# Recurrent branch of a hybrid layer: the product of input gate and convolution output on GpSimd instead of VectorE

## The chip, the cores and the metric

The kernel runs on one core of one Trainium2 chip. The metric is the device time of one execution in microseconds (us). The engines are named as in the profile: PE (TensorE), DVE (VectorE), ACT (ScalarE), POOL (GpSimd), SP (SyncE, which issues the DMAs).

## The reference

One layer on 128 context tokens and 1024 latent tokens, 1152 columns in all: a normalised and modulated input goes through one projection into a pooling branch, a recurrent branch and a gate; the two branches are joined by an output projection; a SwiGLU block follows. The change touches the recurrent branch alone:

```
def rg_lru_bidir(xb, w_a, b_a, w_x, b_x, lam, h0):
    ...
    for d in range(N_DIRS):
        r = jax.nn.sigmoid(... xh, w_a[d] ...)
        i = jax.nn.sigmoid(... xh, w_x[d] ...)
        log_a = LRU_C * r * jax.nn.log_sigmoid(lam[d])
        a = jnp.exp(log_a)
        mult = jnp.sqrt(jnp.maximum(-jnp.expm1(2.0 * log_a), 0.0))
        h = linear_scan(a, mult * (i * xb), h0[:, d], reverse=(d == 1))
        ...
```

The product that is moved is `i * xb`: input gate by convolution output. The width of the branch is 512, in four blocks of 128 partitions, and there are two directions, so there are eight such products of 128x1152 float32.

## The kernel before

Channels lie on the partitions and the 1152 tokens on the free axis. The program is not written in the order in which it runs: each piece of work is put into a list with the engines that may do it and a price in us, and a planner (`Sched.run`, printed in part below) sets the order. At each step it takes, over all engines, the piece that could start first by its prices, and among those that could start at once the one that was listed first; a piece that needs a tile waits until a slot of that tile's tag is free. The result is a fixed order for each engine, which the engine follows instruction by instruction: behind one that waits, everything on that engine waits. The helpers `dve`, `tt`, `act`, `pool` and `pe` put a piece on one engine; `anycopy` and `split` leave the choice between ACT and DVE to the planner. The prices come from formulas (`c_dve`: 1.27 us for a product of 1152 columns) or stand in the call.

The recurrent branch is `lru(j)` for j = 0 to 3 (line 647 on). On DVE and ACT it makes the convolution output `xb` (line 659), splits it into a high and a low part `xh`, `xl` (by `split`, lines 309, 311 and 340), multiplies these with the gate weights on PE (line 527, PSUM tile `pt`), and takes the sigmoids on ACT into four `ri` tiles: `rt[d]`, the recurrence gate, and `it[d]`, the input gate. Then for both directions: `a` and a tanh on ACT, a square `sq` (line 702), a product into `rt[d]` (line 704), and the product `it[d]` by `xb` (a `tt`, shown as line 327). A square root on ACT follows, then `it[d]` by `rt[d]` (line 327), the scans (line 719), and their sum.

Around it PE has other work that the planner puts between: the units of the input projection (`gemm_in`, `full_unit`), the modulation (`mod_group`, line 851), and the pooling units (`pool_unit`, whose products on DVE are tiles `C`, `W`, `mix`, with lines 791, 327, 805 to 818). At about 240 us the output projection begins (`gemm_out_mm`, PSUM tiles `ps` and `pm`, line 527), which needs the split `HT`, `LO` of the finished `mix` tiles.

POOL has little to do: memsets of the edges of the tiles `u`, `X` and `C` (lines 550 to 552, 762 to 764, 790), which wait for a free slot of the tag `u`, and between 59 and 68 us some twenty small operations on 128x8 (lines 628 to 640).

Of the kernel before, what the change touches and what calls it, by code (L numbers as in the profile page):

```python
# [11 lines left out]
OP = mybir.AluOpType  # L12
# [4 lines left out]
T = 1152  # L17
# [239 lines left out]
def c_act(n, ps=False, ptr=0):  # L257
    return (("ACT", cp(n, ps) + 0.093 * ptr),)


def c_dve(n, fast=False, ptr=0):
    return (("DVE", 0.068 + n * (0.52 if fast else 1.042) / 1000 + 0.067 * ptr),)
# [10 lines left out]
def kernel(ctx: ExitStack, tc: tile.TileContext, x, cT, vec, rows, w_modA, w_modB, w_in, w_gate,  # L273
                      w_pool, w_out, w_fi, w_fo, y, st_out):
    nc = tc.nc
# [9 lines left out]
    def sb(name, tag="s", shape=(128, T), dt=F32, n=1):  # L285
        return S.buf(tag, lambda: sp.tile(list(shape), dt, name=name, tag=tag, bufs=counts[tag]), n)
# [13 lines left out]
    def act(dst, src, w, r, func=AF.Copy, n=None, ps=False, tset=None, ptr=0, **kw):  # L300
        def fn(e):
            k = {a: (b() if callable(b) else b) for a, b in kw.items()}
            nc.scalar.activation(dst(), src(), func, **k)  # L303
        return S.op(c_act(n, ps, ptr), fn, r, w, tset)
# [18 lines left out]
    def dve(fn, w, r, n, fast=False, ptr=0):  # L323
        return S.op(c_dve(n, fast, ptr), lambda e: fn(), r, w)

    def tt(dst, a, b, w, r, n, op=OP.mult):
        return dve(lambda: nc.vector.tensor_tensor(dst(), a(), b(), op=op), w, r, n)  # L327
# [7 lines left out]
    def pool(fn, w, r, dur):  # L335
        return S.op((("POOL", dur),), lambda e: fn(), r, w)
# [313 lines left out]
    def lru(j):  # L650
        S.tag = f"lru{j}"
        u = us.pop(j)
        xb = sb("xb")
# [35 lines left out]
        for d in range(2):  # L689
            r, i8 = rt[d], d * 4 + j  # L690
            a = av[d] = sb("a")
            act(lambda a=a, r=r: a.t, lambda r=r: r.t, a.all(), r.all() + [("cl",)], AF.Exp, T, tset=EXP, ptr=1,
                scale=cl[:, i8:i8 + 1])
            act(lambda r=r: r.t, lambda r=r: r.t, r.all(), [("cl",)], AF.Tanh, T, tset=TANH, ptr=1,
                scale=ncl[:, i8:i8 + 1])
            sq = sb("sq")

            def square(e, sq=sq, a=a):
                if e == "ACT":
                    nc.scalar.activation(sq.t, a.t, AF.Square)  # L700
                else:
                    nc.vector.tensor_tensor(sq.t, a.t, a.t, op=OP.mult)
            S.op(c_act(T) + c_dve(T), square, a.all(), sq.all())
            dve(lambda r=r, sq=sq: nc.vector.scalar_tensor_tensor(r.t, sq.t, 1.0, r.t, op0=OP.add, op1=OP.mult),
                r.all(), sq.all(), T)
            ig = it[d]
            tt(lambda ig=ig: ig.t, lambda ig=ig: ig.t, lambda: xb.t, ig.all(), xb.all(), T)
        for d in range(2):
            r = rt[d]
            act(lambda r=r: r.t, lambda r=r: r.t, r.all(), [], AF.Sqrt, T, tset=SQ)  # L710
        for d in range(2):
            r, ig, a, i8 = rt[d], it[d], av[d], d * 4 + j
# [185 lines left out]
    for j in range(4):  # L898
        for m in (j, 4 + j):
            if m not in M0:  # L900
                full_unit(m)
        fin(j, lru(j))
        if j == 0:
            mod_group(1)
# [663 lines left out]
```

## Time and profile before

| what | value |
|---|---|
| median of 3 runs | 1091.04 us (1090.93 to 1091.44) |
| time of the profiled execution | 1091.11 us |
| its span in the trace | 1089.3 us |
| mean granted TensorE clock | 0.996 of full speed |
| PE busy | 1071.3 us, 98% |
| DVE busy | 786.7 us, 72% |
| ACT busy | 463.5 us, 43% |
| POOL busy | 10.4 us, 1% |

The span is the time from the first to the last instruction in the trace; 1.8 us of the profiled execution's time lie around it. The profiled execution is 0.07 us above the median.

The busy time over the span in 40 slices of 27.2 us, in tenths:

```profile
PE   7999999999999999999999999999999999999997
...
DVE  5776888996868986658456575574667977878876
ACT  8576858764754333223233232232323233233341
POOL 0020000000000000000000000000000000000000
```

The branch in question lies in slices 3 to 8 (70 to 226 us). Shares of busy time are averages over stages with different limits; what an engine's time is worth is seen from the chain of waits in a stage.

### The profile page before, as it was taken

The page shows a single profiled execution, that of the slowest core. Times are in us where ns is not written, and L with a number is a line of the kernel's source. Part 1 is how long each engine was busy: PE and PEld are TensorE (multiplying, and loading weights), DVE is VectorE, ACT ScalarE, POOL GpSimd, SP SyncE. Part 2 cuts the span into 40 slices and gives each one's busy share as a digit, 9 for nine tenths or more (in the row PEclk, how much of TensorE's full clock was granted, in tenths as well). Part 3 has the DMA queues.
Part 4 walks back from the last instruction along what each step waited for, and adds up shares of the span by engine and source line. Part 5 has one row for each costly group of instructions (what it writes and reads, how often), then busy time and mean ns, then how long its engine had stood idle before and what let it go on. Part 6 is the DMA issues. An engine that isn't in the chain of part 4 may idle for free.

```text
span 1089.3 us, 14667 instructions
## 1 busy us (share of the span) xinstructions
PE 1071.3 (98%) x5708; PEld 920.0 (84%) x5708; DVE 786.7 (72%) x1363; ACT 463.5 (43%) x814; POOL 10.4 (1%) x54
## 2 busy tenths in 40 slices
PE   7999999999999999999999999999999999999997
PEld 6986899988888998888888888888888888888885
DVE  5776888996868986658456575574667977878876
ACT  8576858764754333223233232232323233233341
POOL 0020000000000000000000000000000000000000
PEclk9999999999999999999999999999999999999999
DMA  9868411224413012214223123141237953353622
GB/s 366 305 211 298 150 46 52 78 87 165 139 75 98 20 73 78 111 39 150 84 67 131 72 98 112 39 150 73 78 131 244 377 180 105 85 178 107 203 68 96
DMA packets 47941, 142.09 MB, mean 130 GB/s; under 512 B 4848, under 2 KB 7808, under 8 KB 47872
## 3 DMA queue, kind: packets, MB, share of 16 engines
q1 hardware_dynamic: 47872, 141.17, 37.5%
q8 instruction: 44, 0.72, 0.3%
q14 instruction: 25, 0.20, 0.1%
HBM read 110.06 MB, written 31.08 MB: 130 GB/s over the span
## 4 chain that ended last, share of the span: by engine, by line
PE 92%; DVE 4%; DMA 2%; issue 1%; ACT 1%; SPq 0%; DVEq 0%
PE ps L527 34%; PE ps L1192 30%; PE pm L527 11%; PE pt L527 8%; PE pt L1192 5%; DMA xt<-in_x 1%; PE pm L851 1%; PE pt L460 1%; DVE W L327 1%; DVE C L791 1%; PE pt L490 1%; DVE ri L719 0%; DMA mraw<-in_w_modB 0%; DVE ri L327 0%; DVE ul L340 0%
## 5 line engine op out<-in xcount | busy, mean ns | idle before, releaser
L527 PE MATMUL ps<-bw,au 128*128 128x512 f32 x627 | 164.1, 390 | 0.0
L527 PEld LDWEIGHTS ps<-bw,au 128*128 128x128 f32 x627 | 117.7, 188 | 25.2
L1192 PE MATMUL ps<-T,wu 128*128 128x512 f32 x480 | 117.2, 393 | 0.0
L1192 PE MATMUL ps<-HT,wu 128*128 128x512 f32 x320 | 106.0, 392 | 0.0
L1192 PEld LDWEIGHTS ps<-T,wu 128*128 128x128 f32 x480 | 88.1, 188 | 18.3
L309 ACT ACTIVATE au<-araw 128x512 fp32r<-128x512 f32 x72 | 45.1, 632 | 131.9 <-PE ps L527 80.5
L527 PE MATMUL ps<-HT,uh 128*128 128x384 f32 x280 | 84.9, 345 | 0.0
L527 PE MATMUL ps<-LO,uh 128*128 128x384 f32 x280 | 82.6, 336 | 0.1
L527 PE MATMUL ps<-HT,ul 128*128 128x384 f32 x280 | 82.6, 336 | 0.0
L1192 PEld LDWEIGHTS ps<-HT,wu 128*128 128x128 f32 x320 | 60.1, 188 | 13.2
L1192 PE MATMUL ps<-LO,wu 128*128 128x512 f32 x160 | 62.4, 390 | 0.0
L303 ACT ACTIVATE g<-g 128x512 f32<-128x512 f32 x40 | 25.3, 632 | 83.4 <-DVE g L327 83.2
L309 ACT ACTIVATE wu<-q 128x512 fp32r<-128x512 f32 x60 | 37.8, 629 | 52.7 <-DVE q L327 49.8
L309 ACT ACTIVATE wh<-rw 128x1024 fp32r<-128x1024 f32 x43 | 45.3, 1056 | 31.7 <-DMA rw<-in_w_fi 19.5
L327 DVE TENSOR_TENSOR wu<-q,wu 128x512 fp32r<-128x512 f32 x80 | 54.9, 686 | 2.7 <-ACT wu L309 1.4
L527 PEld LDWEIGHTS ps<-HT,uh 128*128 128x128 f32 x280 | 51.2, 189 | 5.7 <-issue 5.1
L340 DVE TENSOR_TENSOR wl<-rw,wh 128x1024 fp32r<-128x1024 f32 x44 | 53.6, 1219 | 3.0 <-PE ps L1192 2.6
L527 PE MATMUL pt<-bw,au 128*128 128x512 f32 x198 | 54.8, 389 | 0.0
L340 DVE TENSOR_TENSOR au<-araw,au 128x512 fp32r<-128x512 f32 x77 | 51.8, 685 | 1.7 <-ACT au L309 1.3
L527 PEld LDWEIGHTS ps<-LO,uh 128*128 128x128 f32 x280 | 51.9, 189 | 0.3 <-DVE LO L340 0.3
L527 PEld LDWEIGHTS ps<-HT,ul 128*128 128x128 f32 x280 | 51.8, 189 | 0.0
L1192 PE MATMUL ps<-T,wh 128*128 128x512 f32 x160 | 49.5, 391 | 0.0
(322 smaller groups left out, 2357.5 us busy)
## 6 DMA issues: line engine op xcount, KB each, us to landing
rw<-in_w_fi SPq DMA_DIRECT2D x44, 512.0 KB
mraw<-in_w_modB SPq DMA_DIRECT2D x32, 512.0 KB
gdr<-g SPq DMA_DIRECT2D x20, 576.0 KB
araw<-gdr SPq DMA_DIRECT2D x20, 512.0 KB
xt<-in_x SPq DMA_DIRECT2D x18, 512.0 KB
wm<-in_w_modA SPq DMA_DIRECT2D x16, 512.0 KB
rows<-in_w_fo SPq DMA_DIRECT2D x16, 512.0 KB
araw<-sdr SPq DMA_DIRECT2D x15, 512.0 KB
```

The costliest lines, as they stand in the source:

```text
L303: nc.scalar.activation(dst(), src(), func, **k)
L309: nc.scalar.activation(dst(), src(), AF.Copy)
L327: return dve(lambda: nc.vector.tensor_tensor(dst(), a(), b(), op=op), w, r, n)
L340: dve(lambda: nc.vector.tensor_tensor(l(), src(), h().bitcast(F32), op=OP.subtract), w_l, list(r) + list(w_h), n)
L460: nc.tensor.transpose(pt.t[:, i * 128:(i + 1) * 128], xn.t[:, k * 128:(k + 1) * 128], ident)
L490: nc.tensor.matmul(pm.t[32 * j:32 * j + 32, 0:128], sT[:, kt].rearrange("p a b -> p (a b)"), ws[kt // 2].t[:, kt % 2, kind, kk * 128:(kk + ...
L527: nc.tensor.matmul(out, lhsT, rhs, start=first, stop=last)
L791: dve(lambda: nc.vector.tensor_tensor_scan(C.t[:, 1:], ones.to_broadcast([128, PADW - 1]), X.t[:, :PADW - 1], 0.0, op0=OP.mult, op1=OP.add ...
L851: nc.tensor.matmul(pm.t[32 * j:32 * j + 32, 0:256], sT[:, kt].rearrange("p a b -> p (a b)"), raw.t[:, j * 256:(j + 1) * 256], start=kt == ...
L1192: nc.tensor.matmul(ps.t, w, m, start=first and kt == 0 and i == 0, stop=kt == 3 and i == 2, skip_group_check=not first)
```

## The change

The eight products `it[d]` by `xb` go from DVE to POOL. Nothing else in the text of the kernel differs, but the planner makes its order anew, with a price of 2.4 us on POOL in place of 1.27 us on DVE.

```
             ig = it[d]
-            tt(lambda ig=ig: ig.t, lambda ig=ig: ig.t, lambda: xb.t, ig.all(), xb.all(), T)
+            pool(lambda ig=ig: nc.gpsimd.tensor_tensor(ig.t, ig.t, xb.t, op=OP.mult), ig.all(), xb.all(), 2.4)
```

Inputs and output are the same SBUF tiles of 128x1152 float32 as before.

## Rows read from the trace of the kernel before

**Rows 1.** The page's part 1: busy time of each engine, its share of the span, and its instructions.

```profile
PE 1071.3 (98%) x5708; PEld 920.0 (84%) x5708; DVE 786.7 (72%) x1363; ACT 463.5 (43%) x814; POOL 10.4 (1%) x54
```

**Rows 2.** Busy time by stretches of 40 us from 80 us on: stretch, its length, then busy us and (instructions) of PE, PEld, DVE, ACT and POOL, the granted clock, the DMA share and GB/s. In the stretches between 280 and 1080 us, left out here, PE's busy time is 40.00 in every one. The last row is the sum over 80 to 1120 us.

```profile
80.00:120.00 40.00, 39.62 (x316) 28.48 (x315) 29.42 (x40) 28.03 (x36) 0.40 (x3) 1.00 0.88 298
120.00:160.00 40.00, 40.00 (x244) 37.96 (x243) 33.75 (x39) 27.01 (x37) 0.71 (x1) 1.00 0.14 46
160.00:200.00 40.00, 40.00 (x232) 40.00 (x232) 35.46 (x36) 34.27 (x47) 0.00 (x0) 1.00 0.20 56
200.00:240.00 40.00, 38.37 (x217) 37.16 (x216) 40.00 (x46) 25.28 (x35) 1.29 (x10) 1.00 0.26 77
240.00:280.00 40.00, 39.84 (x179) 33.11 (x178) 28.38 (x43) 21.93 (x37) 0.00 (x0) 1.00 0.40 145
...
sum 1040.00, PE 999.86 PEld 856.43 DVE 733.53 ACT 407.38 POOL 2.40; mean PE 38.46 PEld 32.94 DVE 28.21 ACT 15.67 POOL 0.09
```

**Rows 3.** The chain that ended last, in order of time, from 194 to 243 us: start us, us, engine, tile and line. Between the two ends of this stretch every piece is DVE or "issue".

```profile
194.33 0.44 DVE ph L311
...
239.99 0.47 DVE X L311
240.59 1.85 PE ps L527 x7
```

**Rows 4.** PE's timeline from 218 to 262 us, the rows with idle time in front (in brackets, with what ended it); there are no others in this stretch.

```profile
221.78 0.44 PE L527 MATMUL pt<-ml,ph 128*128 128x384 f32 x1 [1.14 <-DVE ml L340]
...
236.88 0.44 PE L527 MATMUL pt<-ml,ph 128*128 128x384 f32 x1 [0.26 <-DVE ml L340]
...
238.25 0.45 PE L527 MATMUL pt<-mh,ph 128*128 128x384 f32 x1 [0.24 <-ACT mix L303]
...
240.59 0.70 PE L527 MATMUL ps<-uh,HT 128*128 128x512 f32 x2 [0.15 <-DVE X L311]
```

**Rows 5.** The instructions of tile `ri`, the group that the diff moves: count, duration ns min/median/max, first and last start us.

```profile
L327 DVE TENSOR_TENSOR ri<-ri,xb x8: 1350/1352/1359, 93.7 to 195.5; 128x1152 f32<-128x1152 f32 x8
```

**Rows 6.** POOL's timeline: start us, us, line, operation. The first seven are the small products and sums of line 636 and 637 (128x8), the last a memset of one column.

```profile
61.07 0.22 POOL L636 TENSOR_TENSOR sm<-sm 128x8 f32<-128x8 f32 x1
...
61.70 0.21 POOL L636 TENSOR_TENSOR sm<-sm 128x8 f32<-128x8 f32 x1
...
63.24 0.33 POOL L636 TENSOR_TENSOR sm<-sm 128x8 f32<-128x8 f32 x1
63.66 0.42 POOL L637 TENSOR_SCALAR sm<-sm 128x8 f32<-128x8 f32 x1
64.17 0.36 POOL L636 TENSOR_TENSOR sm<-sm 128x8 f32<-128x8 f32 x1
64.61 0.43 POOL L637 TENSOR_SCALAR sm<-sm 128x8 f32<-128x8 f32 x1
65.12 0.35 POOL L636 TENSOR_TENSOR sm<-sm 128x8 f32<-128x8 f32 x1
...
154.69 0.71 POOL L790 MEMSET C<- 128x1 f32 x1 [66.60 <-ACT u L318]
```

**Rows 7.** DVE's timeline beside the first seven rows of the group before: a copy out of PSUM, and four subtractions with both inputs in SBUF.

```profile
61.57 0.88 DVE L477 COPY st<-pt 128x128 f32<-128x128 f32 x4 [1.47 <-PE pt L460]
...
63.42 1.98 DVE L340 TENSOR_TENSOR LO<-st,HT 128x384 fp32r<-128x384 f32 x4
```

**Rows 8.** POOL's memsets by line: shapes, count, busy us, mean ns.

```profile
L764 POOL MEMSET X<- 128x256 f32 x4 | 1.2, 312 | 0.0
...
L763 POOL MEMSET X<- 128x16 f32 x4 | 0.4, 112 | 0.0
```

**Rows 9.** DVE's timeline from 100 to 196 us: five of the eight products (`ri<-ri,xb`), and the rows with idle time in front that follow them; the row at 154.60 stands beside the last row of group 6, and the one at 155.40 before the first gate matmul of the group after this.

```profile
100.06 1.36 DVE L327 TENSOR_TENSOR ri<-ri,xb 128x1152 f32<-128x1152 f32 x1 [3.40 <-ACT ri L303]
...
130.37 0.43 DVE L311 CAST gh<-graw 128x512 fp32r<-128x512 f32 x1 [1.92 <-PE pt L527]
...
131.51 1.35 DVE L327 TENSOR_TENSOR ri<-ri,xb 128x1152 f32<-128x1152 f32 x1
133.49 0.69 DVE L311 CAST uh<-raw 128x1024 fp32r<-128x1024 f32 x1 [0.63 <-PE ps L527]
...
154.60 0.76 DVE L311 CAST xh<-xb 128x1152 fp32r<-128x1152 f32 x1
155.40 1.36 DVE L340 TENSOR_TENSOR xl<-xb,xh 128x1152 fp32r<-128x1152 f32 x1
159.49 0.69 DVE L311 CAST uh<-raw 128x1024 fp32r<-128x1024 f32 x1 [2.74 <-PE ps L527]
...
164.69 1.35 DVE L327 TENSOR_TENSOR ri<-ri,xb 128x1152 f32<-128x1152 f32 x1
...
175.31 1.36 DVE L327 TENSOR_TENSOR ri<-ri,xb 128x1152 f32<-128x1152 f32 x1 [2.28 <-ACT ri L303]
...
182.46 2.63 DVE L327 TENSOR_TENSOR ri<-ri 128x1152 f32<-128x1152 f32 x2 [0.81 <-ACT ri L303]
...
191.59 1.35 DVE L327 TENSOR_TENSOR ri<-ri,xb 128x1152 f32<-128x1152 f32 x1
...
195.47 1.35 DVE L327 TENSOR_TENSOR ri<-ri,xb 128x1152 f32<-128x1152 f32 x1
```

**Rows 10.** PE's timeline: the first gate matmul of lru(2).

```profile
156.87 0.33 PE L527 MATMUL pt<-xh,gh 128*128 128x384 f32 x1
```

## The prediction

> **What bounds the kernel now.** First the page's busy times: PE 98%, DVE 72%, POOL 1% [rows 1]. So a microsecond taken from DVE counts only where PE waits for DVE, and the next view is busy time by stretches [rows 2]. There the reader is to see that PE is full almost everywhere after 80 us: 39.62 of 40 in the first stretch, 38.37 and 39.84 in the two that hold 200 to 280 us, and 40.00 in all others up to 1080. Third, the chain of waits in time [rows 3]: it runs over PE until 194.3, over DVE to 240.6, and over PE again. In that piece DVE is full (40.00 of 40 between 200 and 240, [rows 2]). Last, PE's own timeline there [rows 4]: four gaps of 1.14 + 0.26 + 0.24 + 0.15 = 1.79 us, three of them ended by DVE, one by ACT, which emptied a PSUM tile.
>
> So there is one place where DVE's load sets the end, 194 to 241 us. In front of it PE has other work to put between, and behind it PE is never empty. What the change can gain is bounded by the idle time: 1.79 us, since PE's work is the same and nothing runs faster than a full PE. What it can lose isn't bounded so: each microsecond that DVE comes later in that piece makes PE idle for one more.
>
> **What is removed.** Eight products on DVE of 1.352 us, the first at 93.7, the last at 195.5 [rows 5]: 10.8 us of DVE. Two of them, at 191.59 and 195.47, stand where DVE has no idle time any more (the last gap is the one before 182.46, [rows 9]); six stand earlier.
>
> **What is added: eight products on POOL.** The trace has no POOL operation of this size. From below: a memset takes 312 ns for 256 columns and 112 for 16 [rows 8], so a column costs (312 - 112) / 240 = 0.83 ns, one stream of 1152 columns 0.96 us; with the 0.21 of a whole product of 8 columns [rows 6] that is 1.17 us, if all three streams (two in, one out) run together. From above: all three by turns, 3 x 0.96 + 0.21 = 3.09 us. Two by turns make 2.13. I take 2.4, the price that the diff itself sets, since it is nearest to two inputs that take turns. The GPSIMD Engine Reference of the Trainium skill, section 3.1 (Elementwise), gives 4497 ns for a float32 product or sum of 2048 columns, as an estimate 2.53 us for 1152; no run here shows it, and by it the sum below would be 2.4 us in place of 2.2.
>
> POOL's time itself is hidden: it is 99% idle, and the product is wanted only after the square root on ACT (the second product of lru(2) starts at 175.31, its user at 182.46, [rows 9]).
>
> **What POOL's work costs DVE.** This decides the sign. At 61.07 to 61.70, while DVE copies out of PSUM, a pair of POOL's small operations takes 0.63 us from start to start; from 63.24 to 65.12, while DVE subtracts with both inputs in SBUF, a pair takes 0.94, and POOL starts one every 0.47 where DVE takes 1.98 / 4 = 0.49 for one [rows 6, 7]. POOL goes in step with DVE: one operation in each of DVE's seams. And the memset of one column at 154.69 took 0.71 where others of 16 columns take 0.11 [rows 6, 8]; it ended at 155.40, 0.04 after DVE's cast of 154.60 to 155.36 [rows 9]. So POOL waits out a whole DVE instruction. That DVE waits as long for POOL no row shows, as no POOL operation of before is long. From below it is 0 (they run side by side, and DVE gains its 1.35), from above POOL's whole 3.09. I take the whole 2.4, as the two cases above show a wait to the end of the instruction.
>
> The Trainium skill says the same of the other direction (SBUF — State Buffer, section "Who interferes with whom"): a DVE instruction with two SBUF inputs and a POOL instruction that reads SBUF exclude each other, "whoever issues first" has the ports for the whole instruction, and the other is blocked. The trace agrees for POOL as the one that waits (0.71 for 0.11); for DVE as the one that waits it shows nothing yet. By it each product costs DVE more than it saves; without it the change would be worth up to 1.8 us.
>
> DVE's instructions in this piece (products, splits, scans) have both inputs in SBUF but for the copies out of PSUM, so a cover from other work is rare. A moved product then costs DVE 2.4 - 1.35 = +1.05, plus the 0.04 of a handover: 1.09.
>
> **Which of the eight count.** The one at 100.06 came after 3.40 us in which DVE waited for its own input, so DVE is free while POOL works. The second of lru(1), at 131.51, was followed by a gap before 133.49: without it DVE stands idle for 2.0 us, which covers all but 0.4 of POOL's 2.4. The one at 164.69 costs the 1.05, and the 2.28 of idle time before 175.31 take that up; the one at 175.31 falls in the gap that it caused itself. Before 130.37, 159.49 and 182.46 stand further gaps of 1.92, 2.74 and 0.81 [all rows 9]. So the six earlier products cost nothing and gain nothing at the end. The last two stand in the full piece: 2 x 1.09 = 2.2 us that DVE reaches 240.6 later, and PE's gaps there grow from 1.8 to some 4.0 us. Behind it PE is full and nothing gives the time back.
>
> Sum on the profiled execution: 1089.3 + 1.8 around the span = 1091.1, + 2.2 = 1093.3 us. The median of before is 0.07 lower, so this is +0.2% by either. With the ends of POOL's price the two products cost between 2 x (1.17 - 1.35) = -0.4 and 2 x (3.09 - 1.35) = +3.5 us, so this case reaches from 1090.7 to 1094.6.
>
> **Rivals.**
>
> *Side by side.* POOL's long product reads between DVE's accesses, and DVE loses little or nothing. For it: nothing of before shows a DVE instruction that was lengthened by POOL, and POOL's small operations did go on at DVE's pace. Against it: the lock-step and the memset. DVE then arrives at 240.6 up to 2.7 us earlier and PE's 1.79 go: 1091.1 - 1.8 = 1089.3 at best, faster or no change. It decides if DVE's products beside POOL's keep their 1.35. Chance 0.24.
>
> *The delays add up.* The order of all engines is planned with a DVE that is 10.8 us lighter and with no contention. Where PE's instructions are put close behind DVE's, a late DVE stops PE at once, and PE's lateness comes back to DVE over the sigmoids. For it: the first gate matmul of lru(2) begins at 156.87, 0.11 after the split of 155.40 ends [rows 9, 10]. Against it: the gaps named above. If none of the earlier six is taken up, it is 8 x 1.05 = 8.4 us, 1099.5; half of it is 1095.3. It decides if more than a third of DVE's waits on POOL falls where no gap follows. Chance 0.18, slower.
>
> *The product comes late.* POOL starts only when DVE leaves it a seam, and its user `it[d]` by `rt[d]` waits. For it: the memset of 154.69. Against it: 4 us or more between product and user in each block (175.31 + 2.4 against 182.46). It would cost one DVE instruction in a block whose chain is open, in lru(3): 1.35 us, 1092.5. Chance 0.08.
>
> **How the numbers follow.** My forecast has the rest, 0.50. A measurement of this kernel can tell about 0.2%, 2.2 us, from no change, and the forecast lies on that edge, so its half goes to each side. Faster by over 0.2% (below 1088.9) would need more than PE's 1.79 of idle time, or a luckier order elsewhere: 0.05 out of the first rival. Slower (above 1093.2): 0.25 of the forecast, all of the adding up, a little of the late product, and the plan's own risk, in sum 0.49. No change: the rest, 0.46. The range goes from the first rival's best, 1089.4, to 1098, a good part of the way to the sum of all eight.
>
> **What would show it.** In the profile after: eight POOL rows of 128x1152 of about 2.4 us; beside each a DVE row with two SBUF inputs that is lengthened from 1.35 to as much as 3.7 us; DVE's busy time not 10.8 us lower but some 8 higher; PE's idle time between 200 and 262 us at 4 in place of 1.79, with its chain there still on DVE. Wrong it would be if DVE's rows beside POOL's keep their length (first rival), or if PE has new gaps between 100 and 194 us (second).

## The result, and the profile after

The kernel after took 1098.43 us (median of 4 runs, 1096.91 to 1099.44) against 1091.24 (4 runs) of the kernel before beside it: a ratio of 1.0054, 95% interval [1.0041, 1.0067], so some 5.9 us slower (4.5 to 7.3; the two medians alone differ by 7.2). The forecast was 1093.3, in a range of 1089.4 to 1098.0: the sign was right and the size was not. On the forecast's scale, 1091.1 for the kernel before, the ratio gives 1097.0. The profiled execution took 1097.53 us with a span of 1095.7.

The page's part 1 of the kernel after, which answers to [rows 1]:

```profile
PE 1072.9 (98%) x5708; PEld 921.9 (84%) x5708; DVE 785.5 (72%) x1357; ACT 466.8 (43%) x814; POOL 33.4 (3%) x62
```

POOL has the eight products now (62 instructions in place of 54), and 23 us more of busy time: 8 x 2.75 is 22, and most of the rest is a wait in the last one. DVE has lost eight products of 1.35 us, 10.8 us in all, but its busy time fell by 1.2 only. Not all of that can be read as waiting, since the new order also shares the copies between ACT and DVE in another way. The run e3 below has the same order with no product at all, and its part 1 has 776.1 for DVE:

```profile
PE 1072.3 (98%) x5708; PEld 921.8 (84%) x5708; DVE 776.1 (71%) x1357; ACT 466.3 (43%) x814; POOL 10.4 (1%) x54
```

So beside POOL's products the same DVE instructions take 9.4 us more: a wait for POOL is no idle time in this profile, it stands in the duration of the instruction that waits.

Busy time by stretches of 40 us, the columns of [rows 2]:

```profile
80.00:120.00 40.00, 39.49 (x316) 28.16 (x314) 27.77 (x37) 27.30 (x35) 5.79 (x5) 1.00 0.86 293
120.00:160.00 40.00, 40.00 (x244) 37.55 (x240) 34.12 (x38) 28.08 (x37) 6.63 (x3) 1.00 0.16 56
160.00:200.00 40.00, 40.00 (x233) 40.00 (x232) 28.50 (x29) 33.15 (x42) 8.16 (x3) 1.00 0.12 40
200.00:240.00 40.00, 34.72 (x191) 34.40 (x190) 40.00 (x40) 23.08 (x31) 4.48 (x8) 0.96 0.19 59
240.00:280.00 40.00, 39.23 (x183) 33.43 (x183) 28.69 (x36) 25.10 (x36) 0.40 (x3) 1.00 0.44 153
```

PE lost next to nothing between 80 and 200 us (39.49 for 39.62 in the first row). It has 34.72 in place of 38.37 in the stretch of 200 to 240, where the granted clock is 0.96 in place of 1.00, and it is full again from 280 on as before. DVE is full there, as it was; but in the stretch in front of it DVE's busy time fell by 7, from 35.46 to 28.50. That row was not expected: DVE was idle just ahead of the piece in which it is too slow.

PE's timeline of the kernel after in the piece of [rows 4], the rows with idle time in front:

```profile
227.58 0.69 PE L527 MATMUL pt<-ml,ph 128*128 128x384 f32 x1 [5.29 <-DVE ml L340]
...
245.10 0.45 PE L527 MATMUL pt<-mh,ph 128*128 128x384 f32 x1 [0.77 <-ACT mix L303]
```

The gap behind `ml` grew from 1.14 to 5.29 us; the four gaps of 1.79 became two of 6.06, which is 4.3 more. PE's busy time is 1072.9 in place of 1071.3 for the same 5708 matmuls: 1.6 more. Together that is 5.9 us of the 6.4 by which the span grew; the other 0.5 us are idle time of PE elsewhere, most of it before 120 us. So nearly the whole loss is in this place and in what TensorE's clock did there. The clock by stretches of 5 us (stretch, length, PE's busy us and instructions, granted clock, DMA share, GB/s):

```profile
220.00:225.00 5.00, 2.29 (x14) 1.00 0.11 46
225.00:230.00 5.00, 2.42 (x8) 0.76 0.02 1
230.00:235.00 5.00, 5.00 (x28) 0.90 0.01 3
```

Behind the gap of 5.29 us, part of these stretches ran at 1.2 instead of 2.4 GHz; the first matmul there takes 0.69 us in place of the 0.44 of [rows 4]. The granted clock is the mean over a whole stretch, idle time included, so the share that is missing counts by the length of the stretch: 5.00 x 0.24 + 5.00 x 0.10 = 1.7 us of full clock were lost. That is an upper estimate of the cost, since not every matmul takes twice as long (0.69 for 0.44); the 1.6 us more of PE's busy time agree with it.

Now the products. The rows of tile `ri` of the kernel after, as [rows 5], and POOL's timeline with five of the products and two memsets of one column:

```profile
L707 POOL TENSOR_TENSOR ri<-ri,xb x8: 2666/2754/3625, 94.4 to 210.1; 128x1152 f32<-128x1152 f32 x8
```

```profile
94.38 2.67 POOL L707 TENSOR_TENSOR ri<-ri,xb 128x1152 f32<-128x1152 f32 x1 [5.66 <-ACT ri L303]
100.72 2.72 POOL L707 TENSOR_TENSOR ri<-ri,xb 128x1152 f32<-128x1152 f32 x1 [3.68 <-ACT ri L303]
125.66 2.98 POOL L707 TENSOR_TENSOR ri<-ri,xb 128x1152 f32<-128x1152 f32 x1 [22.21 <-issue]
...
155.94 0.71 POOL L790 MEMSET C<- 128x1 f32 x1 [20.88 <-DVE xb L659]
...
185.37 2.67 POOL L707 TENSOR_TENSOR ri<-ri,xb 128x1152 f32<-128x1152 f32 x1 [5.14 <-ACT ri L303]
...
210.09 3.62 POOL L707 TENSOR_TENSOR ri<-ri,xb 128x1152 f32<-128x1152 f32 x1
...
216.74 0.10 POOL L790 MEMSET C<- 128x1 f32 x1 [3.02 <-DVE mix L818]
```

And DVE's timeline beside them:

```profile
95.92 2.34 DVE L340 TENSOR_TENSOR xl<-xb,xh 128x1152 fp32r<-128x1152 f32 x1 [1.22 <-ACT xh L309]
...
101.79 1.02 DVE L311 COPY mix<-ps 128x384 f32<-128x384 f32 x2 [0.89 <-PE ps L527]
...
126.22 2.69 DVE L878 TENSOR_TENSOR gr<-mr,rows 64x256 f32<-64x256 f32 x1
...
134.41 1.20 DVE L311 CAST uh<-raw 128x1024 fp32r<-128x1024 f32 x1 [1.90 <-PE ps L527]
...
187.97 1.36 DVE L702 TENSOR_TENSOR sq<-a 128x1152 f32<-128x1152 f32 x1 [6.66 <-ACT a L303]
...
211.08 2.66 DVE L805 TENSOR_TENSOR W<-W,vt 128x8 f32<-128x8 f32 x1
...
216.60 1.21 DVE L340 TENSOR_TENSOR ul<-raw,uh 128x1024 fp32r<-128x1024 f32 x1
...
226.18 1.34 DVE L340 TENSOR_TENSOR ml<-mix,mh 128x1152 fp32r<-128x1152 f32 x1
```

In the kernel before, three of these instructions stand in DVE's timeline as follows:

```profile
177.88 1.36 DVE L702 TENSOR_TENSOR sq<-a 128x1152 f32<-128x1152 f32 x1
...
209.13 0.16 DVE L805 TENSOR_TENSOR W<-W,vt 128x8 f32<-128x8 f32 x1
...
220.38 1.35 DVE L340 TENSOR_TENSOR ml<-mix,mh 128x1152 fp32r<-128x1152 f32 x1
```

Read these rows against POOL's. The product of 8 columns at 211.08 took 2.66 us (0.16 in the kernel before) and ended at 213.74, right where POOL's product of 210.09 ended (213.71). The split at 95.92 took 2.34 (1.36 for the same shape in [rows 9]); POOL's product ended at 97.05, and from there to 98.26 are 1.21, nearly a split's own time. The row at 126.22, beside POOL's product of 125.66, took 2.69 (0.42 in the kernel before). So each of these three DVE instructions with two SBUF inputs that came after the start of POOL's product was not done before that product was, as if it had stood still until then. The cast of 134.41, SBUF to SBUF, beside POOL's product of 132.12 to 135.06, was held too (1.20 for the 0.69 of [rows 9]); the two copies out of PSUM at 101.79 went on beside POOL's product of 100.72 to 103.44 at 0.51 each. The split `ml`, the row at 226.18, started at 220.38 in the kernel before: it is 5.8 us later, and it is what PE waits for.

The row at 187.97 shows the other thing: 6.66 us in which DVE waited for ACT's exponential `a`. In the kernel before, the same instruction started at 177.88 with no wait. POOL has no part in it: e3, which has no product on POOL, shows the same wait, with 7.28 us. From this row to the start of `ml` DVE has no marked wait any more, 38.2 us long; in the kernel before, the stretch without one in front of `ml` begins at 182.46 [rows 9] and is 37.9 us long. So of the 5.8 us by which `ml` is late, 5.5 are the later start of that stretch and 0.3 its length.

### The profile page after: what moved, and what is told of

It is laid out like the page before. It is cut to its first block, busy times and chain, and to the rows that moved or that the text cites. A ratio compares the mean times of both kernels' runs of the same rounds, so it can differ in the third digit from the quotient of the medians.

```text
span 1095.7 us, 14663 instructions
## 1 busy us (share of the span) xinstructions
PE 1072.9 (98%) x5708; PEld 921.9 (84%) x5708; DVE 785.5 (72%) x1357; ACT 466.8 (43%) x814; POOL 33.4 (3%) x62
## 4 chain that ended last, share of the span: by engine, by line
PE 93%; DMA 3%; DVE 3%; ACT 1%; issue 0%; SPq 0%; DVEq 0%; ACTq 0%
PE ps L527 36%; PE ps L1192 30%; PE pm L527 11%; PE pt L527 8%; PE pt L1192 5%; DMA xt<-in_x 1%; PE pm L851 1%; DMA mraw<-in_w_modB 1%; PE pt L460 1%; PE pt L490 1%; DVE ri L719 0%; ACT HT L309 0%; DVE e L327 0%; DVE ri L704 0%; DVE W L805 0%
```

## The experiments

After the result, three theories stood against each other for the 3.7 us beyond the forecast: POOL's products cost DVE more than I took (contention); the order that the planner made anew loses by itself, whichever engine computes the products (the plan); TensorE's clock, which falls behind PE's longer gap, takes the rest (the clock). The kernels e1 to e4 ran beside 12 runs of the kernel before (median 1092.39 us), e5, e6, e8 and e9 beside 25 (1092.50), e7, e10 and e11 beside 16 (1092.01), e12 beside 13 (1092.63). "Old order" is the order of the kernel before, "new order" that of the kernel after.

| kernel | order | products | median us | ratio to before [95%] |
|---|---|---|---|---|
| after | new | 8 on POOL | 1098.43 | 1.0054 [1.0041, 1.0067] |
| e1 | new | 8 on DVE | 1097.63 | 1.0049 [1.0037, 1.0061] |
| e3 | new | none | 1094.88 | 1.0028 [1.0017, 1.0039] |
| e2 | old | 8 on POOL | 1096.45 | 1.0040 [1.0028, 1.0052] |
| e5 | old | first 6 on POOL | 1092.65 | 0.9999 [0.9990, 1.0009] |
| e6 | old | last 2 on POOL | 1095.78 | 1.0028 [1.0018, 1.0038] |
| e9 | old | none | 1092.17 | 0.9995 [0.9986, 1.0004] |
| e4 | new, PE kept busy | 8 on POOL | 1099.27 | 1.0065 [1.0052, 1.0077] |
| e11 | old, PE kept busy | last 2 on POOL | 1095.05 | 1.0023 [1.0014, 1.0033] |
| e7 | made with DVE's price of POOL's work | 8 on POOL | 1097.02 | 1.0047 [1.0034, 1.0060] |
| e8 | new, exponential preferred | 8 on POOL | 1106.24 | 1.0123 [1.0109, 1.0137] |
| e10 | new, exponential at once | 8 on POOL | 1103.61 | 1.0100 [1.0088, 1.0112] |
| e12 | made with 1.35 for 1.27 us | 8 on DVE | 1094.54 | 1.0018 [1.0008, 1.0028] |

### The order and the engine, each alone: e1, e2, e3

e1 keeps the new order and computes the products on DVE:

```
-            pool(lambda ig=ig: nc.gpsimd.tensor_tensor(...), ig.all(), xb.all(), 2.4)
+            pool(lambda ig=ig: nc.vector.tensor_tensor(...), ig.all(), xb.all(), 2.4)
```

> The new plan (POOL's price of 2.4 us and the order of all engines that comes of it), but the eight products are issued on DVE, at the places where the plan has them. Contention theory (POOL's products hold DVE up, 2.75 us each against the 1.35 that they save): without POOL's work the loss goes, DVE's longest wait-caused gap on PE falls from 5.3 to 2 us or less, time within 1.5 us of before, 1090 to 1092.5. Plan theory (the new order of PE, ACT and DVE loses the time, since it was made for a DVE that is 10.8 us lighter): most of the loss stays, 1095 or more.

e2 keeps the old order and computes them on POOL:

```
-            tt(lambda ig=ig: ig.t, lambda ig=ig: ig.t, lambda: xb.t, ig.all(), xb.all(), T)
+            dve(lambda ig=ig: nc.gpsimd.tensor_tensor(ig.t, ig.t, xb.t, op=OP.mult), ig.all(), xb.all(), T)
```

> The old plan, unchanged on PE, ACT and SP, but the eight products are issued on POOL, at the places where the plan had them for DVE. Contention theory by the steps of the prediction, with POOL's measured 2.75 us: six products are taken up by gaps, two cost 2 x 1.40 = 2.8 us, 1094; if all eight count, 8 x 1.40 = 11 us, 1102. Plan theory: no loss, 1089.5 to 1092.

e3 keeps the new order and leaves the eight products out (the input gate then doesn't scale `xb`):

```
+            pool(lambda: None, ig.all(), xb.all(), 2.4)
```

> The new plan, and the eight products are left out altogether, so that the output lacks the factor xb: DVE without the 10.8 us and without POOL beside it. Contention theory: PE's gaps between 200 and 262 us shrink to 1 us or less, 1089 to 1091. Plan theory: slower than before even so, 1093 or more.

The forecast of the plan theory held in e1 and e3, and its forecast of no loss failed in e2. Each part alone makes the kernel slower: the new order with nothing on POOL by 0.49%, POOL's products in the old order by 0.40%. Even with no product at all the new order is at +0.28%. Between the kernel after and e1 the medians can't tell (the intervals overlap), so what POOL adds in the new order is read from one place of the traces. The two parts don't add up: 0.49 + 0.40 would be 0.89%, and both together are 0.54%. PE's gap behind `ml` says how they go together. It is 1.14 us in the kernel before [rows 4]; in the three of the new order it stands in PE's timeline as follows, first e3, then e1 (the row of the kernel after stands above):

```profile
224.58 0.69 PE L527 MATMUL pt<-ml,ph 128*128 128x384 f32 x1 [2.78 <-DVE ml L340]
```

```profile
227.90 0.69 PE L527 MATMUL pt<-ml,ph 128*128 128x384 f32 x1 [4.05 <-DVE ml L340]
```

From 2.78 (no products) to 4.05 (on DVE) are 1.27, about one DVE product; from there to 5.29 (on POOL) are 1.24, about a POOL product less a DVE product, 2.75 - 1.35 = 1.40. So in the new order one product counts, not two: the other, at 185.37, falls into DVE's wait of 6.66 us. And from 1.14 to 4.05, 2.9 us, is what the order alone does to this gap; behind it the granted clock of e1 is 0.65 and 0.67 in the stretches of 225 to 230 and 230 to 235 us, at most some 1.7 us of lost clock in each, as estimated above.

### Which products count: e5, e6

Both keep the old order; e5 computes the first six on POOL, e6 the last two:

```
-            tt(lambda ig=ig: ig.t, lambda ig=ig: ig.t, lambda: xb.t, ig.all(), xb.all(), T)
+            dve(lambda ig=ig, v=nc.vector if j == 3 else nc.gpsimd: v.tensor_tensor(ig.t, ig.t, xb.t, op=OP.mult), ig.all(),
+                xb.all(), T)
```

(e6 has `nc.gpsimd if j == 3 else nc.vector`.)

> The old plan with the products of lru(0) to lru(2), six of them, on POOL, and the last two on DVE as before. By the steps of the prediction the six are taken up by DVE's gaps: no change against before, within 1 us. If every product counts with 2.75 - 1.35 = 1.40 us: 8 us slower.

> The old plan with only the two products of lru(3) on POOL. By the steps of the prediction these two carry the whole loss: 2 x 1.40 = 2.8 us, some 3 to 4 us over before with the lowered clock behind PE's longer gap, as much as the old plan with all eight on POOL. If all eight share the loss: a quarter of that, 1 us.

The first six cost nothing (0.9999), and PE's gaps of e5 are those of before. The last two cost +0.28%, and all eight in the same order +0.40% (e2): the intervals overlap, and from the first gate matmul of lru(0) to the end the traces have 1007.7 us for e6 and 1008.0 for e2, so the two carry the loss, or nearly all of it. e6's DVE beside POOL's two products, first POOL's timeline, then DVE's:

```profile
191.88 3.73 POOL L707 TENSOR_TENSOR ri<-ri,xb 128x1152 f32<-128x1152 f32 x1 [35.10 <-ACT ri L303]
196.56 2.79 POOL L707 TENSOR_TENSOR ri<-ri,xb 128x1152 f32<-128x1152 f32 x1 [0.95 <-ACT ri L303]
```

```profile
191.72 1.36 DVE L327 TENSOR_TENSOR ri<-ri 128x1152 f32<-128x1152 f32 x1
193.12 3.71 DVE L327 TENSOR_TENSOR mix<-mix,ri 128x1152 f32<-128x1152 f32 x1
196.75 2.89 DVE L311 CAST ph<-praw 128x512 fp32r<-128x512 f32 x1
```

The product of 193.12 takes 3.71 in place of 1.35, the cast of 196.75, just before which POOL had started its second product, takes 2.89 in place of 0.43: 2.36 + 2.46 = 4.8 us of waiting, less the 2.70 saved, is 2.1 us for the two. The forecast had 2 x 1.09 = 2.2. PE's timeline of e6 shows where they went:

```profile
225.43 0.69 PE L527 MATMUL pt<-ml,ph 128*128 128x384 f32 x1 [3.38 <-DVE ml L340]
...
243.33 0.45 PE L527 MATMUL pt<-mh,ph 128*128 128x384 f32 x1 [0.77 <-ACT mix L303]
```

The gap behind `ml` grew by 3.38 - 1.14 = 2.24, and all gaps there by 2.4. The ratio 1.0028 is 3.1 us, with an interval of 2.0 to 4.2. So the gaps account for it or for most of it; the next pair asks what the clock adds.

### The clock: e4, e11

Behind its gap, e6's granted clock is 0.66 in the stretch of 225 to 230 us; e2's is 0.67, e1's 0.65 and e3's 0.71, behind gaps of 3.46, 4.05 and 2.78 us. Behind the 1.14 of before it stays at 1.00. e4 puts 44 transposes, whose result nobody uses, into PE's gap of the kernel after; e11 puts 28 into that of e6:

```
+                if g == 3 and tg == 0:
+                    for _ in range(44):
+                        nc.tensor.transpose(p.t[:, 384:512], ident, ident)
```

> The changed kernel, with 44 transposes of the identity (some 4.8 us) on PE in front of the first product of the pooling unit before which PE stood idle for 5.3 us; their results are overwritten. Clock theory (PE's granted clock falls to its lower level after that gap, and the work behind it runs at half speed for some us): the clock stays at 1.0 between 220 and 235 us, and 1.5 to 3.5 us come back, 1094.5 to 1097. If the low clock costs nothing: the time of the changed kernel, 1097 to 1099.5, or more if the transposes end late.

> The old plan with the two products of lru(3) on POOL, and 28 transposes of the identity (some 3.0 us) on PE in front of the first product of the pooling unit that PE had to wait 3.4 us for. Clock theory (the lowered clock behind the longer gap costs about 1 us of the 3): the clock stays at 1.0 there, and 0.7 to 1.2 us come back against the same kernel without the transposes. If the clock costs nothing: no change against it.

PE's timeline of e11:

```profile
222.05 3.22 PE L834 MATMUL pt<-ident 128*128 128x128 f32 x28
225.78 0.45 PE L527 MATMUL pt<-ml,ph 128*128 128x384 f32 x1 [0.34 <-DVE ml L340]
```

And a stretch of PE behind its gap, first in e6, then in e11, and a later one in e4:

```profile
225.00:230.00 5.00, 4.57 (x18) 0.66 0.01 1
```

```profile
225.00:230.00 5.00, 4.66 (x28) 1.00 0.03 4
```

```profile
245.00:250.00 5.00, 4.22 (x13) 0.71 0.22 81
```

In e11 the clock is 1.00 from 80 to 1080 us, the first matmul behind the transposes takes 0.45 instead of 0.69, and the median is 0.7 us lower than e6's (1095.05 against 1095.78; 0.5 by the two ratios); the intervals overlap, so 0.7 us is the size that the medians give and not a proven one. In e4 the clock also stays at 1.00 from 200 to 240, but falls to 0.71 in 245 to 250, behind two gaps of 0.77 and 0.73, and the kernel gains nothing (1.0065). So the clock is some 0.7 us of e6's loss (these medians) and up to 1.7 us of the loss of the kernel after (the estimate above), and filling the one gap doesn't reliably give it back.

### What could be had at best: e9

e9 keeps the old order and leaves the eight products out:

```
+            dve(lambda: None, ig.all(), xb.all(), T)
```

> The old plan with the eight products left out altogether, so that the output lacks the factor xb: what the change would be worth if POOL's work were free and the order stayed. By the first rival of the prediction PE's 1.8 us of gaps between 200 and 262 us go: 1 to 2 us faster than before. If DVE isn't the bound there: no change.

0.9995 [0.9986, 1.0004]: with the products gone for nothing, no gain can be told. DVE's timeline of e9 shows why, where the two products of lru(3) had stood without a gap:

```profile
196.57 0.43 DVE L311 CAST ph<-praw 128x512 fp32r<-128x512 f32 x1 [1.26 <-PE pt L527]
...
198.30 0.56 DVE L311 COPY X<-ps 128x384 f32<-128x384 f32 x1 [0.51 <-PE ps L527]
199.22 1.23 DVE L340 TENSOR_TENSOR ul<-raw,uh 128x1024 fp32r<-128x1024 f32 x1 [0.36 <-ACT uh L309]
```

Three new waits, on PE and on ACT, of 2.13 us together take up most of the 2.70 that became free, and 0.57 is left. PE's gap behind `ml` falls only from 1.14 to 0.93. A DVE that is full by the windows can still be late by others' work: take an instruction from it, and here the next limit is 0.6 us away.

### Which detail of the new order: e8, e10, e7, e12

The wait of 6.66 us before 187.97 was the suspect. ACT's timeline of the kernel after:

```profile
180.03 1.10 ACT L303 ACTIVATE ri<-pt,vt 128x384 f32<-128x384 f32 x2 [0.67 <-PE pt L527]
...
185.31 1.28 ACT L303 ACT_TABLE_LOAD   x1
186.61 1.26 ACT L303 ACTIVATE a<-ri,sm 128x1152 f32<-128x1152 f32 x1
```

ACT computes six sigmoids of lru(3), as PE delivers them, and only then the exponential that lru(2) wants. In the kernel before the exponential came first:

```profile
175.30 1.28 ACT L303 ACT_TABLE_LOAD   x1
176.59 1.26 ACT L303 ACTIVATE a<-ri,sm 128x1152 f32<-128x1152 f32 x1
```

e8 makes the sigmoids of lru(3) wait for the exponential, and e10 lets it go at once, with no preference for the table that is loaded:

```
# e8, at the sigmoid and at the exponential
+  [("exp", j)]
+  [("exp", 3)] * (d and j == 2)
# e10, at the exponential
+  tset=None if d and j == 2 else EXP
```

> The changed kernel, but the planner is told that the sigmoids of lru(3) come after the exponentials of lru(2), so that ACT doesn't take six of those sigmoids first. ACT theory (the new plan loses because DVE waits 6.7 us for that exponential): the gap on DVE goes, and what is left is the contention, 1093 to 1096. If that order isn't what the new plan loses by: 1097 to 1099.5.

> The changed kernel, but the planner takes the late exponential of lru(2) without counting its table load, so that it goes ahead of the sigmoids of lru(3). ACT theory (DVE's wait of 6.7 us for it is what the new plan loses by): the gap on DVE goes and 2 to 3 us come back, 1094 to 1097. If the rest of the order decides: 1097 or more.

Both took the wait away and both lost more: +1.23% and +1.00%, e8 beyond both of its forecasts. In e10 the longest wait of DVE there is 1.94 us. In e8 it is 0.66 before the same instruction, but PE waits 4.63 us for DVE in another place; from PE's timeline of e8, in the window of [rows 4]:

```profile
211.35 0.41 PE L527 MATMUL pt<-mh,ph 128*128 128x384 f32 x1 [4.63 <-DVE mh L311]
```

This gap is on `mh`, a split of the same tile, so DVE is late there without the wait of 6.66 us. The late exponential accompanies the loss, but moving it forward by way of the planner doesn't cure it. Both edits also made the rest of the order anew on DVE and ACT, so neither tests the exponential by itself, and no run here does. e7 lets the planner know DVE's price of POOL's work, 2.75 us on DVE; e12 leaves the products on DVE and only raises their price from 1.27 to the measured 1.35:

```
# e7
+            S.op((("DVE", 2.75),), lambda e, ig=ig: nc.gpsimd.tensor_tensor(...), ig.all(), xb.all())
# e12
+            S.op((("DVE", 1.35),), lambda e, ig=ig: nc.vector.tensor_tensor(...), ig.all(), xb.all())
```

> The eight products on POOL, but the planner is told what they cost: it books 2.75 us on DVE for each. Misinformed-plan theory (the new plan loses since it counts on a DVE that POOL then holds up): a plan that knows the price loses less than the changed kernel, 1092 to 1095. If any new plan is as good or bad by chance: anywhere between 1092 and 1106.

> The kernel before, with the eight products on DVE and no POOL in it; only their price in the plan goes from 1.27 to 1.35 us, their measured duration. The planner makes another order from it (PE, ACT and DVE all differ). If the old order is a favourable one and any other loses, whatever gave rise to it: 3 us or more slower than before, 1094 or more. If the loss of the new plan belongs to the lighter DVE that the change announces: within 1.5 us of before.

e7 is as slow as the kernel after (1.0047), and e12, with no POOL product and a price changed by 0.08 us, loses 0.18% [0.08, 0.28], some 2 us, which lies between its two forecasts: its order is another one. The price of 2.4 itself isn't at fault: run by itself, without the chip, the planner makes the same order with any POOL price from 0.5 to 3.6 us. With the products left on DVE at a price of nothing it gives PE, ACT and the DMAs that same order too, so what changes it is that DVE has less to do. Each of the five orders that were made anew (of after, e7, e8, e10 and e12) lost. So among these the order of the kernel before is a favourable one, and the change gave it up; why it is better is not shown. Which detail of the new order loses the 2.9 us is not settled. No kernel here beats the one before; e5 and e9 equal it.

## Why the prediction was right or wrong

*The bound.* Right. "There is one place where DVE's load sets the end, 194 to 241 us", and behind it nothing gives the time back: but for 0.1 us, PE's loss of busy time after 80 us lies in 200 to 280 us.

*The product on POOL.* Taken as 2.4 us with ends of 1.17 and 3.09; measured 2.67 at the least and 2.75 in the middle, in the range and 0.35 above the value taken. The 3.62 of the last one and the 3.73 of e6 hold a wait of their own behind a DVE instruction: in e6 DVE's product ended at 193.08 (start 191.72, 1.36 long), POOL's at 195.61, so 2.53 are left. The estimate by the Trainium skill (GPSIMD Engine Reference, section 3.1 (Elementwise), whose figure is for a sum of two tensors), 2.53 us, was nearer than mine. The shortest whole row is 0.14 above it.

*What it costs DVE.* Right, in mechanism and size: "+1.05, plus the 0.04 of a handover" for each, and e6 shows 2.1 for the two. That the size fits so well is partly luck: DVE waited 2.36 and 2.46 us, near the 2.4 taken for a whole product of POOL, but the products themselves took 2.53 and 2.79. The rows that were missing are there now: 0.16 became 2.66, 0.43 became 2.89. By the Trainium skill (SBUF — State Buffer, section "Who interferes with whom") a DVE instruction with at most one SBUF input doesn't contend with GpSimd outside the modes that use both ports, a cast may use them, and a GpSimd instruction that only writes SBUF doesn't contend with a two-input one. The runs agree on each: the copies out of PSUM kept their 0.51, the casts were held, and the memset at 216.74, inside the split of 216.60, took its 0.10. The memset from which the forecast had drawn the wait, like the one at 155.94 here (0.71), stood beside a cast; as evidence for two-input instructions it was the wrong row, though the conclusion held.

*Which of the eight count.* Right in the old order: e5 at 0.9999, e6 with 2.24 us at PE's gap for the forecast's 2.2. In the new order only one counts.

*The signs.* Two were wrong. DVE's busy time was to be some 8 us higher, as if every product held DVE up; it fell by 1.2, since some products lie beside copies out of PSUM (100.72) or in DVE's own gaps (185.37), where no DVE instruction is lengthened. PE's idle time between 200 and 262 us was to be 4 us and is 6.06.

*The sum.* Wrong, by two terms that it doesn't hold. The step that failed is "the six earlier products cost nothing ... the last two ... 2.2 us", carried over to a kernel whose order isn't the one on which it was worked out. Under the old order it stands; but the change makes the order anew, and that alone costs +0.49% (e1), some 2.9 us of it in PE's gap behind `ml`; the lower clock behind that gap can account for the rest. The forecast had this only as "the plan's own risk", a part of a chance and no term with a price. The rival in which the delays add up named the plan, but by another path: late DVE instructions and new PE gaps between 100 and 194 us. There are none (40.00 of 40 in 120 to 200). The second term is TensorE's clock: the forecast's longer gap was priced at its own length, and behind it the clock falls, for some 0.7 us more in e6 and up to 1.7 in the kernel after. That 1097.0 still lies inside the range is luck: the range's upper end, 1098, was taken from eight products whose delays add up, and they didn't.

*The gain that wasn't there.* The rival "side by side" was priced at up to 1.8 us, all of PE's idle time. e9 takes the products away for nothing and gains at most 0.14%, 1.5 us, by the interval, and 0.05% in the middle: most of DVE's freed time turns into waits on PE and ACT. The change had no upside here that these runs can tell.

*The product comes late.* It didn't: DVE's waits on POOL's result are not among the rows of after or e6; what DVE waits for is that POOL's running product ends.

## What to carry to other kernels

An elementwise product moved to POOL beside a DVE that works on pairs of SBUF tiles cost DVE here nearly the whole POOL duration (2.36 and 2.46 us in e6), less the product that it was spared; look for copies out of PSUM, or for gaps of DVE, to put it beside. Before such a move is priced, leave the work out once and see what that alone would give: here it was nothing that could be told. Where a planner makes the order anew, that is a part of the change with a price of its own, and the engine has to be tried in the old order and the new order with the old engine, each by itself.

## What was not expected of the hardware

The clock of TensorE fell to its lower level for some microseconds behind gaps of PE of 2.78 to 5.29 us, in a kernel that keeps PE at 98% (0.65 to 0.76 of the full clock in the 5 us behind them), which makes such a gap dearer than its length. In e4 it fell behind two gaps of less than 0.8 us, where PE had computed transposes before, so the length of one gap doesn't tell all.

Profiled executions differ by up to 3 us in when the first gate matmul of lru(0) starts (84.4 in the kernel before, 85.0 in after, 86.2 in e6, 87.4 in e4), ahead of anything the edits touch. The granted clock of the first 40 us goes with it in these four: 0.96, 0.96, 0.91 and 0.87; e11, with 0.96 and 86.4, doesn't fit. From there to the end it is 1004.9 us in the kernel before, 1010.7 in after, 1009.7 in e1, 1008.0 in e2, 1007.7 in e6, 1006.9 in e11 and 1004.2 in e9. That is the reason why differences under 2 us are read here from medians of several runs, or from one place of the trace, and not from two spans.
